# Gate and up maps by Strassen's seven block products, the down map spread between them, its last share and the final norm token-major

## The chip, the cores and the metric

The kernel runs on one core of a Trainium2 chip. The metric is the device time of the whole program in microseconds (us). Three runs of the kernel before took 1119.18, 1119.93 and 1120.37 us, so the median is 1119.93 us.

## What is computed

The reference is one inference step of a two-layer streaming encoder. Every layer is `x = x + mixer(norm(x))`, then `x = x + ffn(norm(x))`; a last norm follows. The part that matters here is the feed-forward map, with `D_MODEL` = 1024 and `D_FF` = 2816:

```
def rmsnorm(x, g):
    xf = x.astype(jnp.float32)
    y = xf * lax.rsqrt(jnp.mean(xf * xf, axis=-1, keepdims=True) + EPS)
    return (y * g.astype(jnp.float32)).astype(x.dtype)

def swiglu(x, w_gate, w_up, w_down):
    return (jax.nn.silu(x @ w_gate) * (x @ w_up)) @ w_down
...
        x = x + y
        x = x + swiglu(rmsnorm(x, norm_ffn[layer]), ffn_gate[layer], ffn_up[layer], ffn_down[layer]).astype(x.dtype)
    return (rmsnorm(x, norm_final), ...
```

The mixer of layer 0 is stick-breaking attention beside a recurrent unit; that of layer 1 subtracts the input from trailing means over 2, 4, 8 and 16 tokens and maps them by groups. 512 prompt tokens and 32 sample tokens go through the same weights, 544 tokens in all. Everything is float32.

## The kernel before

The activations stay on chip, features on partitions: `x` is 128 partitions by 8 feature tiles by 544 tokens. TensorE multiplies in a rounded float32 form, so each float32 factor is split into a rounded part and a rest ("hi" and "lo"), and a product is three passes: hi by hi, hi by lo, lo by hi (`mm3`, L146 to L152, all big maps at line L151). A pass is one matmul for each of two halves of the tokens, 272 columns each (`HALVES`, `HN` = 272).

Weights come in blocks of 128 columns by up to 8 feature tiles (`load_w`, L137 to L144): SP, the sync engine's queue, loads `raw` (512 KB for gate and up), ACT copies it to the rounded `whi` (L141), DVE subtracts for `wlo` (L143). There are three buffers of each.

The feed-forward map (`ffn`, L663) takes the 22 tiles of the hidden width in two blocks of 12 and 10. In a block, each tile gets a gate map and an up map (`ffn_in`, L638; 8 feature tiles x 3 passes x 2 halves = 48 matmuls each). DVE scales the sums with the token norms `rs` (L643, L648), ACT does silu, DVE multiplies (L649), and the result is split into `hh` (ACT, L653) and `hl` (DVE, L654). The down map of the block follows: for each of 8 output tiles the sum over the block's hidden tiles, added to `x` by DVE (`add_x`, L594). In layer 1 the last block runs by two parts of the tokens (`LAST`, 288 and 256 columns), and `after1` (L870 on) works on the final norm tile by tile: squares on ACT (L882), transposes to token-major on TensorE (L903), scaling and output transfers at the end (L906 to L911).

Between the maps, `Norm` (L190) prepares the input of the next one: `split` makes `xh` on ACT and `xl` on DVE (L209), `square` the squares on ACT (L201) and their sum on DVE (L202). `rs` (L228) sums over partitions with one-column matmuls (L224), takes root and reciprocal (L81, L178) and spreads the scales over the partitions with TensorE (L186). In the pooling mixer of layer 1, `pool_out` multiplies with band matrices (L820), DVE adds the result to `x` (L823), and `n3.add(m)` follows; the first gate and up maps of layer 1's feed-forward stand between them.

The order of the work is set by a scheduler on every engine, except on TensorE in attention and in the pooling mixer, where it is the order of the code. POOL builds the band matrices (`band`, L699, and the code behind it, in the stage of attention) and loads the pooling weights `pw` (L734).

## Time and profile before

| | |
|---|---|
| median of three runs | 1119.93 us |
| lowest, highest | 1119.18, 1120.37 us |
| span of the profiled execution | 1118.6 us |
| TensorE (PE) busy | 1098.2 us, 98% |
| VectorE (DVE) busy | 542.5 us, 48% |
| ScalarE (ACT) busy | 400.7 us, 36% |
| GpSimd (POOL) busy | 90.9 us, 8% |
| loaded from memory, stored | 94.88 MB, 4.60 MB |

The profile is of one execution. Its span is what the profiler saw between the first and the last instruction, 1118.6 us; the timed runs are 0.6 to 1.8 us longer, and the profiled execution's own time outside the span is not recorded. PEld is TensorE's loading of the stationary operand, which runs beside the matmuls. "Idle before" is the time in which an engine had nothing to do just before the instructions of a row, with what ended it. A TensorE that is busy all the time need not run at its peak, since matmuls are pipelined: the distance between the starts of two matmuls is the pace, not their duration.

### The profile page before, as it was taken

To read this page: it belongs to the slowest core of one execution; us is meant where nothing else is said; L and a number is where in the kernel's file an instruction comes from. 1 tells how busy PE (TensorE), PEld (TensorE's weight loads), DVE (VectorE), ACT (ScalarE), POOL (GpSimd) and SP (SyncE) were. 2 spreads that over 40 slices of the span, in tenths; PEclk is the share of its full clock that TensorE was granted. 3 is DMA by queue.
4 is the path that set the end of the run, shared out by engine and by line. 5 is a ranking of instruction groups with operands and counts; after the bars stand their busy time and mean duration, and the time that the engine had idled before them with its cause. 6 is when DMAs were issued, how large, how long until landed. Compare 5 with 4: busy or idle time off the path is not lost.

```text
span 1118.6 us, 20133 instructions
## 1 busy us (share of the span) xinstructions
PE 1098.2 (98%) x8591; PEld 1072.5 (96%) x8591; DVE 542.5 (48%) x797; ACT 400.7 (36%) x626; POOL 90.9 (8%) x242
## 2 busy tenths in 40 slices
PE   8989999999999999999999999999999999999997
PEld 7978888899999999999999999999999999999997
DVE  6785667654444342344343455544433224444575
ACT  7555555543322222122232344422222112222454
POOL 5162225400000000000000000000000000000000
PEclk8989999999999999999999999999999999999999
DMA  8412222323232323333322340132222333322364
GB/s 226 130 49 67 68 67 79 97 76 95 76 91 80 91 69 88 95 95 94 93 71 60 94 119 23 43 92 83 88 81 71 88 108 89 94 86 64 108 188 126
DMA packets 183977, 100.78 MB, mean 90 GB/s; under 512 B 4215, under 2 KB 180575, under 8 KB 183888
## 3 DMA queue, kind: packets, MB, share of 16 engines
q1 hardware_dynamic: 182352, 96.88, 29.9%
q0 software_dynamic: 1088, 1.56, 0.5%
q8 instruction: 68, 1.11, 0.4%
q10 hardware_dynamic: 448, 1.05, 0.3%
q14 instruction: 21, 0.17, 0.0%
HBM read 94.88 MB, written 4.60 MB: 89 GB/s over the span
## 4 chain that ended last, share of the span: by engine, by line
PE 89%; DVE 4%; issue 4%; POOL 1%; DMA 1%; ACT 1%; SPq 0%; DVEq 0%; POOLq 0%; ACTq 0%
PE acc L151 82%; DVE sB L390 1%; PE acc L786 1%; DMA raw<-in_hyb_w_in_dram 1%; POOL sA L409 1%; PE z L820 1%; PE sm L820 0%; PE sm L427 0%; DVE sA L391 0%; DVE wlo L143 0%; PE sm L418 0%; DVE tr L339 0%; POOL sB L409 0%; PE sm L903 0%; PE sm L328 0%
## 5 line engine op out<-in xcount | busy, mean ns | idle before, releaser
L141 ACT ACTIVATE whi<-raw 128x1024 fp32r<-128x1024 f32 (+2 forms) x196 | 185.1, 946 | 555.4 <-PE acc L151 537.9
L151 PE MATMUL acc<-xh,whi 128*128 128x272 f32 x1728 | 369.2, 295 | 2.4 <-ACT xh L81 2.4
L151 PE MATMUL acc<-xl,whi 128*128 128x272 f32 x1728 | 363.6, 292 | 0.5 <-DVE xl L209 0.5
L151 PE MATMUL acc<-xh,wlo 128*128 128x272 f32 x1728 | 360.6, 290 | 0.0
L151 PEld LDWEIGHTS acc<-xh,whi 128*128 128x128 f32 x1728 | 273.6, 190 | 9.7 <-issue 5.7
L151 PEld LDWEIGHTS acc<-xl,whi 128*128 128x128 f32 x1728 | 274.1, 191 | 1.0 <-DVE xl L209 0.8
L151 PEld LDWEIGHTS acc<-xh,wlo 128*128 128x128 f32 x1728 | 273.7, 189 | 0.1
L143 DVE TENSOR_TENSOR wlo<-raw,whi 128x1024 fp32r<-128x1024 f32 (+2 forms) x196 | 211.6, 1081 | 91.9 <-ACT whi L141 89.2
L151 PE MATMUL acc<-hh,wlo 128*128 128x272 f32 (+2 forms) x704 | 158.9, 288 | 0.0
L151 PE MATMUL acc<-hl,whi 128*128 128x272 f32 (+2 forms) x704 | 158.8, 288 | 0.0
L151 PE MATMUL acc<-hh,whi 128*128 128x272 f32 (+2 forms) x704 | 158.7, 288 | 0.0
L151 PEld LDWEIGHTS acc<-hl,whi 128*128 128x128 f32 x704 | 115.4, 188 | 0.0
L151 PEld LDWEIGHTS acc<-hh,whi 128*128 128x128 f32 x704 | 115.2, 188 | 0.2 <-issue 0.2
L151 PEld LDWEIGHTS acc<-hh,wlo 128*128 128x128 f32 x704 | 115.2, 188 | 0.1
L648 DVE TENSOR_TENSOR sB<-acc,rs 128x544 f32<-128x544 f32 x44 | 31.9, 725 | 170.3 <-PE acc L151 170.3
L643 DVE TENSOR_TENSOR sA<-acc,rs 128x544 f32<-128x544 f32 x44 | 31.9, 725 | 122.5 <-PE acc L151 118.4
L594 DVE TENSOR_TENSOR x<-x,acc 128x544 f32<-128x544 f32 x32 | 23.1, 721 | 84.1 <-PE acc L151 84.1
L390 DVE TENSOR_TENSOR_SCAN sB<-sB 128x128 f32<-128x128 f32 (+4 forms) x34 | 30.7, 907 | 31.2 <-POOL sB L409 30.8
L653 ACT ACTIVATE hh<-sA 128x544 fp32r<-128x544 f32 x44 | 29.0, 660 | 39.4 <-DVE sA L649 39.4
L775 POOL TENSOR_TENSOR pst<-x,cols 128x120 f32<-128x120 f32 x2 | 1.7, 881 | 444.2 <-DVE x L594 444.2
L654 DVE TENSOR_TENSOR hl<-sA,hh 128x544 fp32r<-128x544 f32 x44 | 31.7, 720 | 5.8 <-ACT hh L653 5.8
L649 DVE TENSOR_TENSOR sA<-sA,sB 128x544 f32<-128x544 f32 x44 | 31.9, 724 | 3.6
(298 smaller groups left out, 901.7 us busy)
## 6 DMA issues: line engine op xcount, KB each, us to landing
raw<-in_ffn_gate_dram SPq DMA_DIRECT2D x44, 512.0 KB, 3.7
raw<-in_ffn_up_dram SPq DMA_DIRECT2D x44, 512.0 KB, 3.8
raw<-in_ffn_down_dram SPq DMA_DIRECT2D x48, 320.0 KB, 3.2
raw<-in_ffn_down_dram SPq DMA_DIRECT2D x32, 384.0 KB, 3.4
raw<-in_hyb_w_in_dram SPq DMA_DIRECT2D x20, 512.0 KB, 3.8
raw<-in_hyb_w_out_dram SPq DMA_DIRECT2D x8, 512.0 KB, 4.1
sA<-in_x_prompt_dram SPq DMA_DIRECT2D x3, 512.0 KB, 4.4
vc<-in_cache_sb_v_dram SPq DMA_DIRECT2D x4, 256.0 KB, 7.1
```

Source lines behind the costliest of these rows:

```text
L141: ac.activation(hi[:, :nk], raw[:, :nk], AF.Copy)
L143: ve.tensor_tensor(lo[:, :nk], raw[:, :nk], hi[:, :nk].bitcast(F32), op=ALU.subtract)
L151: pe.matmul(ps[:, h, : s.stop - s.start], lhsT=a[:, wi, :], rhs=b[:, s], start=first and j == 0, stop=last and j == 2)
L390: ve.tensor_tensor_scan(r, r, r, 1.0, op0=ALU.mult, op1=ALU.min)
L409: gp.affine_select(t[:, N - P :], t[:, N - P :], pattern=[[-1, P]], compare_op=ALU.is_gt, fill=fill, base=0, channel_multiplier=1)
L594: ve.tensor_add(half(x[:, m]), half(x[:, m]), ps[:, :, :HN])
L643: ve.tensor_mul(half(t[0]), ps[:, :, :HN], half(nin.r))
L648: ve.tensor_mul(half(t3), ps[:, :, :HN], half(nin.r))
L649: ve.tensor_mul(t1, t1, t3)
L653: ac.activation(a, t1, AF.Copy)
L654: ve.tensor_tensor(b, t1, a.bitcast(F32), op=ALU.subtract)
L786: pe.matmul(o, lhsT=l[:, c : c + n], rhs=r, start=k % 2 == 0 and j == 0, stop=k % 2 == 1 and j == 2)
```

## The change

The hidden tiles are taken in 11 pairs. For a pair, the weights of gate (and of up, in the same tiles, `u` = 0 and 1) are seen as 2 x 2 blocks: two hidden tiles by two halves of the 8 feature tiles. The activations are 2 x 2 blocks too: two halves of the features by two halves of the tokens. Strassen's scheme makes the four blocks of the result from seven block products instead of eight. The factors are sums of blocks:

- Of the weights: `a11`, `a12`, `a22` are plain blocks; `t1` and `t3` are two blocks added by the transfer itself (a load on SP, then an adding load issued by POOL onto the same tile, L814 and L816 of the new file); `t2` and `t4` are added by DVE (L824). All seven are split into hi and lo (ACT L799, DVE L801).
- Of the activations: class `Forms` makes seven forms for each norm, instead of one split; `put` splits a form into its rounded part (ACT, L288, L291) and its rest (DVE, L289, L292).

A product is 4 feature tiles x 3 passes = 12 matmuls of 272 columns (L905) for gate and for up; a pair has 7 x 12 x 2 = 168. The kernel before had 192. The sums of products are formed in the accumulators, with copies by ACT (L912 to L918) and by DVE from L916 to L936.

The down map no longer waits for a block: after products 3 to 10 of a pair come eight sums (`one`, L961), each over the four hidden tiles finished last, for one output tile and one half of the tokens, added to `x` in 272 columns (L964). The last four hidden tiles of layer 0 follow after the last pair, with the next norm; those of layer 1 are multiplied the other way round (`final`): hidden tiles stationary, weight rows of 512 columns moving, tokens on partitions, on top of `x` transposed into the accumulator. The final norm then is a square with sum over the row, a root, and one scaling.

Weights now live in 17 slots of 128 x 1024, taken and given back by a list that counts products; the adding loads and DVE's sums use slots as well. The order on TensorE is that of the code in all of the feed-forward map: the token norms of layer 0 stand before the fifth product of the first pair (gate and up counted apart), those of layer 1 after the sixth, `t2` by `n2`. The band matrices are built in the second pair, and memory pools are laid out anew.

Two kernels in numbers: 8372 matmuls before, 7762 now.

The core of the diff, in pieces. `after1` and the code of the old final norm are removed and not shown:

```diff
+    class Forms(Norm):
+        names = ("b11", "n1", "n2", "b21", "t3", "t4", "b22")
+        def __init__(self, gcol, t0):
+            super().__init__(gcol)
...
+        def add(self, k):
+            j, g = k % 4, col(self.gcol + k)
+            x0, x1 = x[:, k, :HN], x[:, k, HN:]
+            if k < 4:
+                if j % 2 == 0:
+                    self.d[j], self.d[j + 1] = self.tmp(j // 2)
+                d = self.d[j]
+                self.put("b11", j, x0, g)
+                ve.tensor_tensor(d, x0, x1, op=ALU.subtract)
+                self.put("n1", j, d, g)
+            else:
+                d, g0 = self.d[j], col(self.gcol + j)
+                (t, q), (r, _) = self.tmp(2 + 2 * (j % 3)), self.tmp(3 + 2 * (j % 3))
+                ac.activation(t, x1, AF.Copy, scale=g)
+                ve.scalar_tensor_tensor(q, d, g0, t, op0=ALU.mult, op1=ALU.add)
+                self.put("n2", j, q, -1.0)
+                self.put("b21", j, x0, g)
+                ve.scalar_tensor_tensor(r, x[:, j, HN:], g0, t, op0=ALU.mult, op1=ALU.subtract)
+                self.put("t3", j, r, -1.0)
+                ve.scalar_tensor_tensor(q, x0, g, q, op0=ALU.mult, op1=ALU.subtract)
+                self.put("t4", j, q, -1.0)
+                self.put("b22", j, t)
+            self.square(k)
...
+        def split(self, n, *drop):
+            def go():
+                raw = self.raw[n]
+                hi = slot(f"h{n[0]}", F32R)
+                ac.activation(hi, raw, AF.Copy)
+                lo = slot(f"l{n[0]}", F32R)
+                ve.tensor_tensor(lo, raw, hi.bitcast(F32), op=ALU.subtract)
+                self.w[n] = hi, lo
+                self.free(drop, max(self.at[n], clock.pop(), clock.pop()) + 16)
+            self.steps.append((2, go))
+        def blocks(self, n, *which):
+            def go(t):
+                for b, (f, kh) in enumerate(which):
+                    for u, src in enumerate((ffn_gate, ffn_up)):
+                        w = src[self.l][512 * kh : 512 * (kh + 1), P * f : P * (f + 1)].rearrange("(k p) m -> p k m", p=P)
+                        if b:
+                            gp.dma_start(v(t)[:, u], w, accum_op=ALU.add)
+                        else:
+                            nc.sync.dma_start(v(t)[:, u], w)
+                return len(which)
+            self.load(n, go)
+        def add(self, n, a, b, *drop):
+            def go():
+                t = self.raw[n] = slot(f"r{n[0]}")
+                ve.tensor_add(t, self.raw[a], self.raw[b])
+                self.at[n] = max(self.at[a], self.at[b], clock.pop()) + 8
+                self.free(drop, self.at[n])
+            self.steps.append((1, go))
+        def pair(self, fp):
+            n = lambda s: (s, fp)
+            f0, f1 = 2 * fp, 2 * fp + 1
+            self.blocks(n("t1"), (f1, 0), (f1, 1))
+            self.blocks(n("a11"), (f0, 0))
+            self.split(n("a11"))
+            self.split(n("t1"))
+            self.add(n("t2"), n("t1"), n("a11"), n("t1"), n("a11"))
+            self.rows(fp)
+            self.split(n("t2"))
+            self.blocks(n("t3"), (f1, 0), (f0, 0))
+            self.blocks(n("a12"), (f0, 1))
+            self.split(n("a12"))
+            self.add(n("t4"), n("t2"), n("a12"), n("t2"), n("a12"))
+            self.split(n("t3"), n("t3"))
+            self.blocks(n("a22"), (f1, 1))
+            self.split(n("a22"), n("a22"))
+            self.split(n("t4"), n("t4"))
...
+    ORDER = (("a11", "b11"), ("t1", "n1"), ("t2", "n2"), ("a12", "b21"), ("t3", "t3"), ("a22", "t4"), ("t4", "b22"))
...
+            a, b = ORDER[i]
+            (wh, wl), (bh, bl) = [v(w) for w in sup.need((a, fp))], nin.form(b)
+            X, Y = st["xy", u][:, 0, :HN], st["xy", u][:, 1, :HN]
+            Z = st["z", u][:, :HN] if i else None
+            o = (X, Z, X, Y, X, X, Z)[i]
+            first = i in (0, 1, 3)
+            mms = [m for k in range(4) for m in ((wh[:, u, k], bh[:, k]), (wh[:, u, k], bl[:, k]))]
+            mms += [(wl[:, u, k], bh[:, k]) for k in range(4)]
...
+            for n, (lt, r) in enumerate(mms):
+                pe.matmul(o, lhsT=lt, rhs=r, start=first and n == 0, stop=n == 11, skip_group_check=True)
+            if u:
+                sup.done((a, fp))
+            pa, pb, pc = st["abc", u]
+            s, out = st["s"], st["u" if u else "s"]
+            h0, h1 = slice(0, HN), slice(HN, T)
+            if i == 0:
+                ac.activation(pa, X, AF.Copy)
+            elif i == 2:
+                ac.activation(pb, X, AF.Copy)
+            elif i == 3:
+                ve.tensor_tensor(out[:, 0, h0], Y, pa, op=ALU.add)
+            elif i == 4:
+                ac.activation(pc, X, AF.Copy)
+                ve.scalar_tensor_tensor(out[:, 1, h1], Z, -1.0, pc, op0=ALU.mult, op1=ALU.subtract)
+            elif i == 5 and u == 0:
+                ve.scalar_tensor_tensor(s[:, 1, h0], X, -1.0, nin.r[:, h0], op0=ALU.mult, op1=ALU.mult)
+                ve.tensor_mul(s[:, 1, h1], s[:, 1, h1], nin.r[:, h1])
+                act(s[:, 1], s[:, 1], AF.Silu)
+                ve.tensor_mul(s[:, 1], s[:, 1], nin.r)
+            elif i == 5:
+                ve.scalar_tensor_tensor(out[:, 1, h0], X, -1.0, s[:, 1, h0], op0=ALU.mult, op1=ALU.mult)
+                ve.tensor_mul(out[:, 1, h1], out[:, 1, h1], s[:, 1, h1])
+                hidden(out[:, 1], 1)
+            elif i == 6:
+                ve.tensor_tensor(out[:, 0, h1], Z, pb, op=ALU.add)
+                if u == 0:
+                    ve.tensor_mul(s[:, 0], s[:, 0], nin.r)
+                    act(s[:, 0], s[:, 0], AF.Silu)
+                    ve.tensor_mul(s[:, 0], s[:, 0], nin.r)
+                else:
+                    ve.tensor_mul(out[:, 0], out[:, 0], s[:, 0])
+                    hidden(out[:, 0], 0)
...
+            def one(m, hf, s):
+                c = slice(P * (m % 4), P * (m % 4 + 1))
+                ps = small()[:, :HN]
+                for i, f in enumerate(fs):
+                    (wh, wl), (a, b) = sup.row(f, m // 4), hid[f]
+                    for j, (lt, r) in enumerate(((wh, a), (wh, b), (wl, a))):
+                        pe.matmul(ps, lhsT=lt[:, c], rhs=r[:, s], start=i == 0 and j == 0,
+                                  stop=i == len(fs) - 1 and j == 2)
+                xs = x[:, m, s]
+                ve.tensor_add(xs, xs, ps)
...
+                if hf:
+                    if fp == PAIRS:
+                        after(m)
...
+        for fp in range(PAIRS):
+            if fp or not first:
+                prods, sums = strassen(sup, nin, fp, hid), down(fp)
+                for n, f in enumerate(prods):
+                    if n == 4 and fp < len(mid):
+                        mid[fp]()
+                    f()
+                    if n > 2 and sums:
+                        sums.pop(0)()
+        if last:
+            last()
+        if after:
+            for f in down(PAIRS):
+                f()
+        return hid
...
-        first = [], []
-        fg, fu = ffn_in(1, n3, 0, *first)
+        first = {}
+        prods = strassen(supply, n3, 0, first)
         for m in range(4, KD):
             pool_out(m)
+            if m == 7:
+                give(*ptm, *ptb)
+                supply.fill()
             if m in (4, 6):
                 pool_state(m == 6)
-            for s in (fg[m - 4], fu[m - 4]):
-                s()
...
+            prods.pop(0)()
+        prods.pop(0)()
+        prods.pop(0)()
+        scales(n3)
+        for f in prods:
+            f()
...
+        def begin(t):
+            s, _ = TT[t]
+            n = s.stop - s.start
+            if t in (0, 3):
+                fin[t] = small(), small()
+            else:
+                a = accp()
+                fin[t] = a[:, 0], a[:, 1]
+            for m in range(KD):
+                pe.matmul(fin[t][m // 4][:n, P * (m % 4) : P * (m % 4 + 1)], lhsT=x[:, m, s], rhs=ident, is_transpose=True,
+                          start=m % 4 == 0, stop=False, skip_group_check=True)
+        def add(t, fs, stop):
+            s, _ = TT[t]
+            n = s.stop - s.start
+            for h in range(2):
+                for i, f in enumerate(fs):
+                    (wh, wl), (a, b) = sup.row(f, h), hid[f]
+                    for j, (lt, r) in enumerate(((a, wh), (b, wh), (a, wl))):
+                        pe.matmul(fin[t][h][:n], lhsT=lt[:, s], rhs=r, start=False,
+                                  stop=stop and i == len(fs) - 1 and j == 2, skip_group_check=True)
+        def out(t):
+            s, dst = TT[t]
+            n = s.stop - s.start
+            y = slot("y")
+            q = fss[:n, 3 * t : 3 * t + 3]
+            for h in range(2):
+                ac.activation(y[:n, 512 * h : 512 * (h + 1)], fin[t][h][:n], AF.Square, accum_out=q[:, h : h + 1])
+            ve.tensor_add(q[:, 2:3], q[:, 0:1], q[:, 1:2])
+            act(q[:, 2:3], q[:, 2:3], AF.Sqrt, bias=eps[:n], scale=1.0 / D)
+            ve.reciprocal(q[:, 2:3], q[:, 2:3])
+            for h in range(2):
+                c = slice(512 * h, 512 * (h + 1))
+                ve.scalar_tensor_tensor(y[:n, c], fin[t][h][:n], q[:, 2:3], grow[:n, c], op0=ALU.mult, op1=ALU.mult)
+                (ac if h else nc.sync).dma_start(dst[:, c], y[:n, c])
+            give(y)
...
+        phase("sqrt_and_others")
+        for t in range(3):
+            begin(t)
+            add(t, fs[:-1], False)
+        for t in range(3):
+            add(t, fs[-1:], True)
+            out(t)
+        for t in range(3, 5):
+            begin(t)
+            add(t, fs, True)
+            out(t)
+    with tc.manual_schedule(engines={mybir.EngineType.PE}):
+        final(supply, ffn(supply, n3, first=first))
```

Two places show how instructions move. The first is DVE in the middle of layer 0's feed-forward map. Before, one hidden tile (`wlo` is the rest of a weight block, `sA`, `sB`, `hl` are the hidden tile's):

```order
L143 TENSOR_TENSOR wlo_584_4239<-raw_582_4235,whi_583_4237 128x1024
L654 TENSOR_TENSOR hl_568_4111<-sA_561_4049,hh_567_4110 128x544
L643 TENSOR_TENSOR sA_573_4169<-acc_569_4114,rs_480_3251 128x544
L143 TENSOR_TENSOR wlo_589_4297<-raw_587_4293,whi_588_4295 128x1024
L648 TENSOR_TENSOR sB_578_4227<-acc_574_4172,rs_480_3251 128x544
L649 TENSOR_TENSOR sA_573_4169<-sA_573_4169,sB_578_4227 128x544
```

Now, a part of one pair (`lt1` is the rest of `t1`, `rt1` the tile that the adding load writes, `rt2` the raw sum `t2`, `l3` a rest of the down map's rows, `s` and `u` the pair's gate and up):

```order
L916 TENSOR_TENSOR u_691_4700<-acc_696_4718,a_697_4719 128x272
L964 TENSOR_TENSOR x_128<-x_128,sm_718_4897 128x272
L824 TENSOR_TENSOR rt2_716_4892<-rt1_704_4742,ra11_707_4774 128x1024
L801 TENSOR_TENSOR lt1_715_4890<-rt1_704_4742,ht1_714_4888 128x1024
L919 SCALAR_TENSOR_TENSOR s_690_4699<-z_705_4748,c_695_4704 128x272
L964 TENSOR_TENSOR x_128<-x_128,sm_719_4925 128x272
L922 TENSOR_TENSOR s_690_4699<-s_690_4699,rs_519_3336 128x272
L919 SCALAR_TENSOR_TENSOR u_691_4700<-z_706_4761,c_699_4721 128x272
L964 TENSOR_TENSOR x_128<-x_128,sm_723_4959 128x272
L801 TENSOR_TENSOR l3_721_4953<-r3_717_4894,h3_720_4951 128x1024
```

The adds to `x` and the combining of products now stand in one queue behind `rt2` and `lt1`, which read what the adding load wrote.

The second place is DVE at the end of layer 1's pooling mixer, from its last feature tile to the token norms (the two reciprocals, `rt`). Before (`nacc` is the sum of squares, `xl` the rest of the activations):

```order
L823 SCALAR_TENSOR_TENSOR x_122<-z_951_7642,cols_121,x_122 128x272
L823 SCALAR_TENSOR_TENSOR x_122<-sm_952_7643,cols_121,x_122 128x272
L209 SCALAR_TENSOR_TENSOR xl_954_7653<-x_122,cols_121,xh_953_7652 128x544
L202 TENSOR_TENSOR nacc_894_7272<-nacc_894_7272,nsq_955_7656 128x544
L178 RECIPROCAL rt_958_7703<-rt_958_7703 128x4
```

Now the last 12 of the 25 rows from the last adds to `x` to the last rest of the form `n2` (`t3`, `t4`, `b22` are rests of other forms, `tmp` sums of them; `lt1` and `rt2` belong to the second pair):

```order
L292 SCALAR_TENSOR_TENSOR n2_1128_7991<-tmp_1160_8107,n2_1127_7990 128x272
L313 SCALAR_TENSOR_TENSOR tmp_1147_8052<-x_128,cols_127,tmp_1147_8052 128x272
L292 SCALAR_TENSOR_TENSOR t3_1132_8000<-tmp_1161_8108,t3_1131_7999 128x272
L801 TENSOR_TENSOR lt1_1181_8212<-rt1_1175_8185,ht1_1180_8210 128x1024
L824 TENSOR_TENSOR rt2_1182_8214<-rt1_1175_8185,ra11_1176_8190 128x1024
L308 SCALAR_TENSOR_TENSOR tmp_1168_8158<-tmp_1118_7949,cols_127,tmp_1168_8158 128x272
L311 SCALAR_TENSOR_TENSOR tmp_1169_8159<-x_128,cols_127,tmp_1168_8158 128x272
L289 TENSOR_TENSOR b22_1135_8008<-tmp_1168_8158,b22_1135_8008 128x272
L218 TENSOR_TENSOR nacc_1095_7715<-nacc_1095_7715,nsq_1170_8174 128x544
L313 SCALAR_TENSOR_TENSOR tmp_1160_8107<-x_128,cols_127,tmp_1160_8107 128x272
L292 SCALAR_TENSOR_TENSOR t4_1134_8005<-tmp_1147_8052,t4_1133_8004 128x272
L292 SCALAR_TENSOR_TENSOR n2_1128_7991<-tmp_1168_8158,n2_1127_7990 128x272
```

The second pair's weight work and the rests of `t3` and `t4` now stand ahead of the last `n2`, which the products `t2` by `n2` read.

## Rows read from the trace of the kernel before

**Rows 1.** Page, part 1: span; busy us, share and count of each engine
```profile
span 1118.6 us, 20133 instructions
...
PE 1098.2 (98%) x8591; PEld 1072.5 (96%) x8591; DVE 542.5 (48%) x797; ACT 400.7 (36%) x626; POOL 90.9 (8%) x242
```

**Rows 2.** Page, part 4: chain of waits by line
```profile
PE acc L151 82%; DVE sB L390 1%; PE acc L786 1%; DMA raw<-in_hyb_w_in_dram 1%; POOL sA L409 1%; PE z L820 1%; PE sm L820 0%; PE sm L427 0%; DVE sA L391 0%; DVE wlo L143 0%; PE sm L418 0%; DVE tr L339 0%; POOL sB L409 0%; PE sm L903 0%; PE sm L328 0%
```

**Rows 3.** Chain of waits in order: start us, us, engine, tile, line, count
```profile
279.45 389.67 PE acc L151 x3087
...
712.69 344.33 PE acc L151 x2706
```

**Rows 4.** Windows, mid feed-forward: busy us (count) per engine; PEclk, DMA share, GB/s
```profile
600.00:640.00 40.00, 40.00 (x321) 40.00 (x320) 16.90 (x24) 14.04 (x20) 0.00 (x0) 1.00 0.29 81
```

**Rows 5.** Timeline of PE, two stretches: start us, us, engine line op out<-in
```profile
1059.76 0.29 PE L151 MATMUL acc<-hh,wlo 128*128 128x288 f32 x1
...
1061.62 0.30 PE L151 MATMUL acc<-hl,whi 128*128 128x288 f32 x1
...
1083.76 0.28 PE L151 MATMUL acc<-hh,whi 128*128 128x256 f32 x1
...
1085.89 0.28 PE L151 MATMUL acc<-hh,whi 128*128 128x256 f32 x1
```

**Rows 6.** Lines by form: op out<-in count | busy us, mean ns | idle before
```profile
L143 DVE TENSOR_TENSOR wlo<-raw,whi 128x1024 fp32r<-128x1024 f32 x116 | 141.7, 1224 | 24.3 <-ACT whi L141 21.9
...
L648 DVE TENSOR_TENSOR sB<-acc,rs 128x544 f32<-128x544 f32 x44 | 31.9, 725 | 170.3 <-PE acc L151 170.3
...
L202 DVE TENSOR_TENSOR nacc<-nacc,nsq 128x544 f32<-128x544 f32 x21 | 15.1, 718 | 0.0
...
L823 DVE SCALAR_TENSOR_TENSOR x<-z,cols,x 128x272 f32<-128x272 f32 x8 | 4.0, 497 | 2.1 <-PE z L820 1.9
...
L681 DVE TENSOR_TENSOR x<-x,acc 128x288 f32<-128x288 f32 x8 | 3.6, 445 | 2.0 <-PE acc L151 2.0
...
L734 POOL DMA_DIRECT2D pw<-in_pool_w_dram x4 | 3.0, 761 | 11.5 <-PE z L529 11.5
```

**Rows 7.** DMA issues: out<-in queue op count, KB each, median us to landing
```profile
raw<-in_ffn_gate_dram SPq DMA_DIRECT2D x44, 512.0 KB, 3.7
...
pw<-in_pool_w_dram POOLq DMA_DIRECT2D x4, 256.0 KB, 4.9
...
out_dram<-sA ACTq DMA_DIRECT2D x2, 256.0 KB, 3.2
```

**Rows 8.** Chain of waits, end of layer 1's pooling mixer
```profile
702.14 0.54 PE sm L799 x4
702.68 1.51 PE acc L151 x12
704.19 0.43 PE z L820 x4
...
705.64 4.72 PE acc L151 x36
```

**Rows 9.** Windows, from the pooling mixer into the feed-forward map of layer 1
```profile
688.00:700.00 12.00, 12.00 (x94) 11.05 (x94) 10.21 (x19) 7.08 (x12) 1.04 (x2) 1.00 0.03 8
700.00:712.00 12.00, 11.43 (x93) 10.97 (x92) 6.52 (x13) 4.95 (x10) 1.00 (x2) 1.00 0.03 6
712.00:724.00 12.00, 12.00 (x83) 11.79 (x84) 5.56 (x7) 5.78 (x8) 0.00 (x0) 0.86 0.28 82
```

**Rows 10.** Timeline, token norms of layer 1 (idle before and its releaser in brackets)
```profile
711.76 1.28 ACT L75 ACT_TABLE_LOAD   x1
711.87 0.82 PE L186 MATMUL z<-ident,rt 128*128 128x128 f32 x5 [0.57 <-DVE rt L178]
```

**Rows 11.** Timeline, end of the program
```profile
1110.09 0.28 PE L151 MATMUL acc<-hh,wlo 128*128 128x256 f32 x1
...
1113.51 1.01 ACTq L911 DMA_DIRECT2D out_dram<-sA  x2
```

More of the change, by code (lines that the diff above doesn't have):

```diff
@@ L267 @@
     rsv = half(rs)
-    kcs = [big.tile([P, 512], F32, tag=f"kc{i}", name=nm("kc")) for i in range(2)]
+    kcs = [lp.tile([P, 512], F32, tag=f"kc{i}", name=nm("kc")) for i in range(2)]
     bdr, bdi = [t.rearrange("p (c o) -> p c o", c=4) for t in kcs]
@@ L363 @@
                           cache_k[0, 0, P * t : P * (t + 1)].rearrange("t h d -> t (h d)"))
[L364 removed]
+    vc = [lp.tile([P, 512], F32, tag=f"vc{t}", name=nm("vc")) for t in range(4)]
     for t in range(4):
@@ L632, with fb, slot @@
     v_out()
+    lg.__exit__(None, None, None)
+    lp2 = ctx.enter_context(tc.tile_pool(name="lp2", bufs=1, side="left", reuse_waits="tile"))
+    def fb(i, n):
+        return lp2.tile([P, 2176 if i == 12 else 1088], F32, tag=f"fb{i}", name=nm(n))
+    spare, held = [(0, i) for i in range(6)], {}
+    clock = [0]
+    def slot(n, dt=F32):
+        spare.sort()
+        when, i = spare.pop(0)
+        t = (sl if i < 6 else sl2).tile([P, 1024], dt, tag=f"w{i}", name=nm(n))
+        held[id(t)] = t, i
+        clock.append(when)
+        return t
@@ L777 @@
     a2 = n2.acc
-    ptm = [scr(("sA", "sA", "sA", "sB", "sB")[t]) for t in range(5)]
+    ptm = [slot("ptm") for t in range(5)]
+    supply = Supply(1)
+    supply.fill()
     def pool_in(pi, t, i):
```

411 lines of the change are left out of this document (227 added, 184 removed).

## The prediction, made before the changed kernel ran

> **What bounds the kernel now.** I read the page's first part, then the chain of waits, then windows of the feed-forward stretches, then the two places where the order of work changes. TensorE is busy 1098.2 of 1118.6 us, and VectorE 542.5 [rows 1]. A high busy share alone can be a stalled pipeline, so the chain matters more: 82% of it is one line, L151, the big maps [rows 2], and it runs through both feed-forward maps in two unbroken pieces [rows 3]. In the window from 600 to 640 us TensorE is never idle at the full granted clock (2.4 GHz), while VectorE is busy 16.90 of 40 us and the DMA engines 0.29 [rows 4]. There the time is a number of matmuls times a pace: 389.67 / 3087 = 0.126 us in layer 0, 344.33 / 2706 = 0.127 us in layer 1 [rows 3]. I take 0.127. What is removed there is worth its full time, as long as VectorE and the transfers keep up.
>
> **The saving.** 192 gate and up matmuls a pair become 168, so 24 x 11 pairs x 2 layers = 528 fewer, all of 272 columns: 528 x 0.127 = **-67.1 us**. Weight loads fall by as many, since there is one for each matmul before and after (x8591 of both in [rows 1]), so the pace should not change.
>
> **The last share of layer 1.** Its matmuls had 288 and 256 columns. 15 starts of the one kind lie 1.86 us apart, 0.133 each; 19 of the other 2.13 us, 0.118 [rows 5]. That is 0.00046 us a column, so 512 columns are estimated at 0.118 + 256 x 0.00046 = 0.236. Before: 576 x 0.127 + 240 x (0.133 + 0.118) = 133.4 us for the whole down map. Now 18 hidden tiles the old way, 864 x 0.127 = 109.7, and 5 token tiles x 2 halves x 4 hidden tiles x 3 passes = 120 x 0.236 = 28.3: 138.0, so +4.6. The 40 transposes stay 40. The way out is 1118.6 - 1110.4 = 8.2 us after the last product [rows 11]; the new one (two squares, root, reciprocal, two scalings of 512 columns, a 256 KB store of 3.2 us [rows 7]) should be about a microsecond shorter. Together **+3.5** (0 to 6).
>
> **Steady pairs, cover by VectorE.** A pair is 168 products and 96 down matmuls, 264 x 0.127 = 33.5 us of TensorE. VectorE gets, at row prices [rows 6]: 9 rests of 128x1024 (seven, and two of down rows) and 2 sums at 1.22, 8 adds to x and 10 combinations of 272 columns at 0.45 (the 288-column row), 6 operations of 544 at 0.725: 13.5 + 8.0 + 4.4 = 25.9 us, 77% of the pair. It fits, but no longer loosely. The adds to x release the two accumulators that the down sums alternate between, so a VectorE that waits more than some 3 us stops TensorE.
>
> What can make it wait is the adding load, an operation that the trace does not have. The loop is: the rest of `t4` is made and frees a slot; SP loads the plain blocks of the next `t1` into it; POOL adds the others; then `rt2` and `lt1` may run; and between these and the next rest of `t4` VectorE has 10 operations of 1024, 6 of 544 and 11 of 272 columns, 12.2 + 4.4 + 5.0 = 21.6 us. So base load plus adding load may take 33.5 - 21.6 = **11.9 us** before the loop, not TensorE, sets the pair. The base is 3.7 us (512 KB from SP, here two of 256 KB) [rows 7]. For the adding loads the lower bound is the same 3.7, the nearest row of POOL's own queue is `pw`: 256 KB, 0.76 us of POOL each to issue [rows 6] and 4.9 us to land [rows 7]. Upper bound: the two after one another, 9.8. So 7.4, 8.6 or 13.5 us; I take two that overlap, 0.8 + 4.9, hence 9.4 with the base, inside the loop by 2.5 us. Transfers grow too: seven block loads of 0.5 MB and about 1 MB of down rows a pair, 4.5 MB in 33.5 us, 134 GB/s beside the 81 of [rows 4], and each adding load also reads its target; latencies may stretch. I put **+2.5** on twenty pairs.
>
> The trace has 4.9 us for a 256 KB load that POOL issues [rows 7]. The Trainium skill, "DMA: Bandwidth & Descriptors" (section "Anatomy of one DMA"), gives such transfers a fit of 2.0 us plus the bytes over 436 thousand a microsecond, 2.6 us here as an estimate, well under the row; by it base and adding load would be some 7 us and the loop loose; the steady term would be 0 and the sum 1083.8. The row decides. Against the change speaks the same page's "Rules for kernel authors": an accumulating DMA reads its destination and writes it later, and only GpSimd can issue it; no run yet shows what that costs.
>
> **First pair of layer 0: +6** (2 to 12). Before, the token norms lay between products that were ready. Now they stand at a fixed place; their chain costs TensorE what it does at layer 1, 0.57 us for the reciprocal [rows 10] and as much for the sums; a table load of 1.28 us [rows 10] delays ACT's copy of `t2`; the first `t3` waits for an adding load that stands in POOL's queue with the band matrices; and the forms are new VectorE work just there. About 1.4 + 0.8 + 2 + 1.3, rounded up for a clock that may drop.
>
> **End of layer 0: +1.5** (0 to 4). An output tile of the last share is now 24 matmuls, 3.0 us, instead of 60. VectorE has two adds, a rest of 0.79, the squares' sum 0.72 and in the later tiles a `pwl` of 0.7 for each, 3.1 us. It ends a little late.
>
> **From the pooling mixer into layer 1: +20** (8 to 27). This is the expensive place. In the kernel before VectorE is already busy 10.21 of 12 us there [rows 9], and TensorE loses little, 0.57 us, and 0.14 of the next 12 us to the clock [rows 9, 10]. Now VectorE's queue holds, from the sum `rt4` to the last rest of `n2`, 36 operations: 7 of 1024 columns at 1.22, 3 sums of squares at 0.72, and 26 of 272 at 0.50 (the L823 row) [rows 6]: 8.6 + 2.2 + 13.0 = 23.7 us. TensorE has in the same stretch a state transpose of 0.54, a product 1.51, `pool_out` 705.64 - 704.19 = 1.45, and another product 1.51 [rows 8]: 5.0 us. It must then wait for `n2`, 18.7 us if VectorE starts no earlier; I take 16.5, since some rows can run ahead, 1.4 for the norms, and 2.1 for the clock: after a pause of half a microsecond it was granted 0.86 over 12 us [rows 9], and this pause is far longer. The adding load for the second pair ends in 9.4 us after the last `pool_out`, earlier than VectorE reaches its rest, so it does not decide here.
>
> **Sum.** -67.1 + 3.5 + 2.5 + 6 + 1.5 + 20 = -33.6. From the profiled 1118.6 us: 1085.0. The median of the runs lies 1.3 us above the span: **1086 us**.
>
> **Rivals.**
> 1. Everything beside the two norms hides: the forms are made early because VectorE has gaps before the mixer ends, and the steady term is 0. For it: 48% busy overall [rows 1]. Against: 10.21 of 12 just there [rows 9]. Then -67.1 + 3.5 + 3 + 7 = -53.6: **1066**.
> 2. The loop is a little too long in the steady pairs: base and adding load 12.5 to 13.3 us, excess 0.6 to 1.4 x 20 pairs = 12 to 28 us on top of the forecast less its 2.5: **1096 to 1112**. For it: the upper bound of 13.5; against: two loads in different halves of a slot need not queue.
> 3. Slower than before: the same loop, longer. It breaks even at an excess of (33.6 + 2.5) / 20 = 1.8 us, at 13.7 us for base plus adding load. At 15.5 us the pair is 3.6 us too long, 72 - 36 = +36: **1156**. For it: an operation without any row, on a queue whose only larger loads take 4.9 us, with targets that must be read too. Against: nothing in the rows is above 13.5.
> 4. The change does not do what it says: the pace per matmul rises because each weight is loaded for one product of 272 columns and the accumulators alternate more often. Against: one weight load for each matmul already. The feed-forward maps keep some 5700 matmuls; at 0.133 us they cost 34 us more, and nothing is gained: **1120**.
>
> **How the numbers follow.** The forecast 0.45 (1074 to 1096), rival 1 0.22, rival 2 0.17, rival 3 0.12, rival 4 0.04. No change means within 0.2%, 2.2 us, about what a measurement of this kernel can tell. Faster is the first three, 0.84; rival 4 straddles and gives 0.03 to the same; slower 0.13. The range goes from 1064, under rival 1, to 1118, over rival 2: it leaves out rival 3 and little else.
>
> **What would show it.** In the profile after: PE around 0.127 us a matmul and idle under 1 us in 40 in the steady pairs, with VectorE near 77%; a gap of some 16 us on TensorE ended by a rest of `n2` on VectorE after layer 1's last `pool_out`; adding loads of about 5 to 6 us. Wrong: gaps of some microseconds in every pair, ended by adds to x, with VectorE itself waiting for a DMA into `rt1` (rivals 2 and 3); or no gap at the mixer's end (rival 1); or a pace above 0.13 without gaps (rival 4).

## The result, and the profile after

The changed kernel took 1206.5 us (median of four runs), 1.078 times the kernel before (95% interval 1.076 to 1.080). The forecast was 1086 us, with a range up to 1118: it was wrong in sign. Rival 3, the loop through the adding loads, comes nearest, with 1156, but not by its sum: it needed 15.5 us for the two loads in the loop, and they took 10.2 (below).

The page after: span and busy time, the granted clock and the DMA share in 40 slices, the queue of POOL's transfers (packets, MB, share of 16 engines' span), and the chain of waits by engine and by line. It answers to [rows 1] and [rows 2]. Below it are the clock and the chain by engine of the kernel before.

```profile
span 1206.0 us, 19831 instructions
PE 1084.3 (90%) x7971; PEld 1036.7 (86%) x7971; DVE 762.9 (63%) x1214; ACT 496.2 (41%) x825; POOL 209.8 (17%) x331
...
PEclk8989999998898999999989899689888999899999
DMA  8322233308464655566644421254645556466422
...
q0 software_dynamic: 47696, 25.16, 16.2%
...
PE 51%; DMA 20%; DVE 14%; issue 7%; ACT 5%; POOL 1%; SPq 1%; DVEq 0%; POOLq 0%; ACTq 0%
PE acc L905 18%; PE sm L961 14%; PE acc L167 9%; DMA rt<-in_ffn_up_dram 9%; DMA ra<-in_ffn_up_dram 7%; DMA r<-in_ffn_down_dram 3%; PE z L905 3%; DVE la L801 2%; DVE lt L801 2%; PE acc L1222 1%; DVE rt L824 1%; ACT ha L799 1%; DVE sB L473 1%; PE acc L1112 1%; DVE l L801 1%
```

```profile
PEclk8989999999999999999999999999999999999999
...
PE 89%; DVE 4%; issue 4%; POOL 1%; DMA 1%; ACT 1%; SPq 0%; DVEq 0%; POOLq 0%; ACTq 0%
```

TensorE fell from 98% to 90% busy [rows 1], and its clock, full in the kernel before through both feed-forward maps but for one stretch [rows 9], now drops again and again from the tenth slice on. In the chain, TensorE's share is 51% (89% before) and transfers hold 20%, among them `rt`, the tiles of the adding loads. The windows show the same by stage: nine pairs of layer 0, the end of the pooling mixer, and ten pairs of layer 1 (us, busy time and count by engine; then clock, DMA share, GB/s).

```profile
317.00:656.00 339.00, 309.77 (x2328) 305.31 (x2329) 213.27 (x318) 120.04 (x170) 46.64 (x36) 0.95 0.56 125
751.00:777.00 26.00, 12.83 (x56) 11.36 (x54) 20.79 (x37) 14.60 (x28) 2.65 (x2) 0.63 0.41 96
785.00:1151.00 366.00, 332.48 (x2490) 327.89 (x2488) 227.72 (x338) 129.99 (x184) 49.85 (x39) 0.94 0.55 123
```

In these pairs TensorE is idle 29 + 34 = 63 us, and the clock takes 0.05 x 339 + 0.06 x 366 = 39 us more. Before, both were zero in such a window [rows 4]. VectorE, at 63% (213.27 / 339), is not full. What ended TensorE's waits (total us, times, longest), the two largest entries of each window, layer 0 first:

```profile
PE acc L905 <- ACT c L918: 8.5, 3, 3.5
PE sm L961 <- ACT hh L942: 8.5, 4, 2.9
...
PE sm L961 <- ACT hh L942: 13.5, 5, 3.2
PE acc L905 <- DVE u L916: 7.8, 3, 5.2
```

With the rests `hl`, 29 of the 63 us end with a hidden tile; most of the others end with a copy or a combination of products (`c`, `u`).

A pair should take 33.5 us. I read it off the starts of VectorE's first combination of each pair (L916): from the fourth to the eleventh pair of layer 0 it is 655.5 - 391.7 = 263.8 us, 37.7 a pair on average. The pairs alternate: 36.5, 42.3, 33.1, 40.9, 33.1, 41.9 and 36.0 us. The chain of waits through the long pair of 42.3 us (start us, us, what) shows two adding loads one after the other:

```profile
431.12 0.45 DVE x L964
...
432.40 5.82 DMA rt<-in_ffn_up_dram
...
439.27 0.39 ACT c L918
439.70 2.57 PE acc L905 x12
...
449.40 5.50 DMA rt<-in_ffn_up_dram
...
460.88 0.82 PE sm L961 x2
```

The first (`t1`) lands at 438.2. ScalarE's copy of it stands ahead of the copy `c`, and the product that waits for `c` starts at 439.7. The second (`t3`) lands at 454.9; its copy and one more on ScalarE stand ahead of the hidden tile's steps, and TensorE waits for that tile (`hh`, `hl`) until 460.9. TensorE at these two places:

```profile
439.70 1.66 PE L905 MATMUL acc<-t,ha 128*128 128x272 f32 x8 [2.61 <-ACT c L918]
...
459.80 0.39 PE L961 MATMUL sm<-hh,h 128*128 128x272 f32 x1 [2.87 <-ACT hh L942]
```

Windows just behind each wait show what the clock then takes: the granted clock is 0.59 and 0.50, with TensorE busy all the time.

```profile
439.70:443.50 3.80, 3.80 (x19) 3.80 (x20) 2.72 (x6) 0.23 (x1) 0.00 (x0) 0.59 0.73 214
...
461.00:464.20 3.20, 3.20 (x14) 3.20 (x15) 1.31 (x2) 0.00 (x0) 0.00 (x0) 0.50 0.27 77
```

The timeline of VectorE and SP around the first load (idle before, and what ended it, in brackets):

```profile
426.72 1.22 DVE L801 TENSOR_TENSOR lt<-rt,ht 128x1024 fp32r<-128x1024 f32 x1
...
428.00 0.37 SPq L816 DMA_DIRECT2D rt<-in_ffn_gate_dram  x1
...
438.31 1.23 DVE L824 TENSOR_TENSOR rt<-rt,ra 128x1024 f32<-128x1024 f32 x1 [6.76 <-DMA rt<-in_ffn_up_dram]
...
444.90 1.23 DVE L801 TENSOR_TENSOR l<-r,h 128x1024 fp32r<-128x1024 f32 x1 [2.48 <-ACT h L799]
...
460.74 1.22 DVE L801 TENSOR_TENSOR lt<-rt,ht 128x1024 fp32r<-128x1024 f32 x1
```

At 426.7 VectorE makes the rest of `t4`, which frees a slot; at 428.0 SP loads the plain blocks; at 438.3, after 6.76 us of idling, VectorE may add `rt2`; at 460.7 comes the next rest of `t4`. This is the loop of the forecast, in this turn 34.0 us long: 10.3 us of loads and 23.7 us in VectorE's queue, where the forecast had 21.6 us of work and no waits (2.48 us for a copy at 444.9 is one). In each of the seven turns between 390.6 and 648.3 SP's load follows the rest of `t4` within 0.1 us. But the turns take 36.2, 34.0, 39.8, 34.2, 38.7, 35.3 and 39.7 us: one of 34.0 alone would cost half a microsecond. In the next one, of 39.8 us, the second adding load stands in the loop as well. It lands at 494.2, VectorE then makes the rest of `t3`, and the rest of `t4` comes behind it:

```profile
495.69 1.23 DVE L801 TENSOR_TENSOR lt<-rt,ht 128x1024 fp32r<-128x1024 f32 x1 [1.95 <-ACT ht L799]
...
500.52 1.23 DVE L801 TENSOR_TENSOR lt<-rt,ht 128x1024 fp32r<-128x1024 f32 x1
...
501.82 0.37 SPq L816 DMA_DIRECT2D rt<-in_ffn_gate_dram  x1
```

From the landing of `t1` at 472.1 to the end of that rest it is 29.7 us.

### The profile page after: what moved, and what is told of

Same layout as the page of the kernel before. It is cut to its first block, busy times and chain, and to the rows that moved or that the text cites. A ratio compares the mean times of both kernels' runs of the same rounds, so it can differ in the third digit from the quotient of the medians.

```text
span 1206.0 us, 19831 instructions
## 1 busy us (share of the span) xinstructions
PE 1084.3 (90%) x7971; PEld 1036.7 (86%) x7971; DVE 762.9 (63%) x1214; ACT 496.2 (41%) x825; POOL 209.8 (17%) x331
## 3 DMA queue, kind: packets, MB, share of 16 engines
q0 software_dynamic: 47696, 25.16, 16.2%
HBM read 124.76 MB, written 4.60 MB: 107 GB/s over the span
## 4 chain that ended last, share of the span: by engine, by line
PE 51%; DMA 20%; DVE 14%; issue 7%; ACT 5%; POOL 1%; SPq 1%; DVEq 0%; POOLq 0%; ACTq 0%
PE acc L905 18%; PE sm L961 14%; PE acc L167 9%; DMA rt<-in_ffn_up_dram 9%; DMA ra<-in_ffn_up_dram 7%; DMA r<-in_ffn_down_dram 3%; PE z L905 3%; DVE la L801 2%; DVE lt L801 2%; PE acc L1222 1%; DVE rt L824 1%; ACT ha L799 1%; DVE sB L473 1%; PE acc L1112 1%; DVE l L801 1%
## 5 line engine op out<-in xcount | busy, mean ns | idle before, releaser
L961 PE MATMUL sm<-hh,h 128*128 128x272 f32 x640 | 192.0, 300 | 39.4 <-ACT hh L942 30.5
L961 PE MATMUL sm<-hl,h 128*128 128x272 f32 x640 | 191.3, 299 | 8.2 <-DVE hl L943 8.2
L961 PE MATMUL sm<-hh,l 128*128 128x272 f32 x640 | 189.1, 295 | 1.3 <-DVE l L801 1.3
L814 POOL DMA_DIRECT2D rt<-in_ffn_gate_dram x44 | 56.7, 1289 | 651.0 <-PE z L905 210.6
L799 ACT ACTIVATE ht<-rt 128x1024 fp32r<-128x1024 f32 x88 | 91.3, 1053 | 183.5 <-DMA rt<-in_ffn_up_dram 176.2
L961 PEld LDWEIGHTS sm<-hh,h 128*128 128x128 f32 x640 | 125.7, 196 | 44.8 <-ACT hh L942 33.1
L801 DVE TENSOR_TENSOR lt<-rt,ht 128x1024 fp32r<-128x1024 f32 x88 | 108.6, 1234 | 43.4 <-ACT ht L799 40.9
L961 PEld LDWEIGHTS sm<-hl,h 128*128 128x128 f32 x640 | 126.1, 197 | 10.9 <-DVE hl L943 10.9
L961 PEld LDWEIGHTS sm<-hh,l 128*128 128x128 f32 x640 | 126.1, 197 | 1.5 <-DVE l L801 1.5
L964 DVE TENSOR_TENSOR x<-x,sm 128x272 f32<-128x272 f32 x176 | 75.7, 431 | 68.7 <-PE sm L961 68.5
L905 PE MATMUL acc<-b,ha 128*128 128x272 f32 x704 | 107.4, 296 | 9.6 <-DVE u L926 9.2
L905 PEld LDWEIGHTS acc<-b,ha 128*128 128x128 f32 x704 | 97.1, 195 | 10.8 <-DVE u L926 9.9
L801 DVE TENSOR_TENSOR la<-ra,ha 128x1024 fp32r<-128x1024 f32 x66 | 80.5, 1222 | 28.8 <-ACT ha L799 23.2
L801 DVE TENSOR_TENSOR l<-r,h 128x1024 fp32r<-128x1024 f32 x44 | 53.9, 1224 | 68.4 <-ACT h L799 65.1
L799 ACT ACTIVATE ha<-ra 128x1024 fp32r<-128x1024 f32 x66 | 69.7, 1058 | 63.5 <-DMA ra<-in_ffn_up_dram 53.7
L824 DVE TENSOR_TENSOR rt<-rt,ra 128x1024 f32<-128x1024 f32 x44 | 54.2, 1232 | 65.1 <-DMA rt<-in_ffn_up_dram 48.2
L799 ACT ACTIVATE h<-r 128x1024 fp32r<-128x1024 f32 x44 | 46.6, 1059 | 111.8 <-DMA r<-in_ffn_down_dram 107.0
L167 PE MATMUL acc<-xh,whi 128*128 128x272 f32 x320 | 75.7, 318 | 2.3 <-ACT xh L97 2.3
L814 POOL DMA_DIRECT2D rt<-in_ffn_up_dram x44 | 74.6, 1695 | 14.2 <-DMA rt<-in_ffn_up_dram 13.1
L905 PE MATMUL acc<-n,ht 128*128 128x272 f32 x352 | 63.2, 329 | 10.9 <-ACT n L291 6.6
L167 PE MATMUL acc<-xl,whi 128*128 128x272 f32 x320 | 68.4, 295 | 0.5 <-DVE xl L227 0.5
L167 PE MATMUL acc<-xh,wlo 128*128 128x272 f32 x320 | 67.9, 294 | 0.0
```

Of the source, the lines that this page charges most:

```text
L167: pe.matmul(ps[:, h, : s.stop - s.start], lhsT=a[:, wi, :], rhs=b[:, s], start=first and j == 0, stop=last and j == 2)
L799: ac.activation(hi, raw, AF.Copy)
L801: ve.tensor_tensor(lo, raw, hi.bitcast(F32), op=ALU.subtract)
L814: gp.dma_start(v(t)[:, u], w, accum_op=ALU.add)
L824: ve.tensor_add(t, self.raw[a], self.raw[b])
L905: pe.matmul(o, lhsT=lt, rhs=r, start=first and n == 0, stop=n == 11, skip_group_check=True)
```

## The experiments

Four groups ran on one chip each: late_sums to slots18, gate to ve_sums_gate, second_plain and ve_sums_gate_rs, and the last two. The chip of the changed kernel's first runs is not on record. The kernel before is the same everywhere within 0.2%; the changed one is not, as the last group shows, so where a few us matter I compare within a group or say that the chips differ. "Pair" is the mean from the fourth to the eleventh pair of layer 0.

| kernel | median us | ratio to before | pair us |
|---|---|---|---|
| changed | 1206.5 | 1.078 (1.076 to 1.080) | 37.7 |
| late_sums | 1216.6 | 1.089 (1.083 to 1.095) | 38.9 |
| no_add | 1153.9 | 1.029 (1.026 to 1.031) | 35.4 |
| late_no_add | 1124.1 | 1.004 (1.003 to 1.006) | 34.1 |
| slots18 | 1209.0 | 1.080 (1.077 to 1.083) | 37.6 |
| gate | 1214.1 | 1.086 (1.083 to 1.089) | 38.5 |
| ve_sums | 1114.7 | 0.996 (0.995 to 0.998) | 33.1 |
| pool_sums | 1125.0 | 1.005 (1.004 to 1.007) | 33.7 |
| ve_sums_gate | 1107.7 | 0.990 (0.987 to 0.993) | 33.1 |
| second_plain | 1162.7 | 1.038 (1.036 to 1.039) | 35.6 |
| ve_sums_gate_rs | 1112.8 | 0.994 (0.993 to 0.995) | 33.1 |
| after_again | 1216.9 | 1.086 (1.085 to 1.088) | 38.7 |
| gate_again | 1211.6 | 1.082 (1.080 to 1.083) | 38.2 |

**late_sums**

```diff
-                    if n > 2 and sums:
+                    if n > 5 and sums:
```

> The eight sums of the down map start after the seventh product of a pair (gate and up counted apart) instead of the fourth; nothing else changes. Two theories. A, two causes: in every odd pair the first sum reads hidden tiles that VectorE and ScalarE finish only some 8 us after the last product of the pair before, since rests of weight blocks stand between; in the changed kernel TensorE waits about 40 us in all for hh and hl (21 in layer 0, 19 in layer 1), and each wait is followed by a stretch at half clock, about half of the 53 us that the clock cost in both feed-forward maps. A expects these waits to vanish: 1206 - 40 - 25 = about 1140. B, one cause: the loop through the adding load and VectorE's queue is longer than a pair, and the waits for hh are only the place where the lag shows. B expects the waits to move to other products and the time to stay above 1185.

No gain: 1216.6. The waits for `hh` fell from 31 to 4 us, but waits for the copy `b` on ScalarE took their place (46.5 us), and from the fifth pair on all are now about 38 us long. The chain at one of them:

```profile
563.50 1.02 PE z L905 x8
564.53 3.06 DMA rt<-in_ffn_gate_dram
568.16 0.89 POOL rt L814
569.04 5.53 DMA rt<-in_ffn_up_dram
574.65 1.07 ACT ht L799
575.75 1.24 DVE lt L801
577.00 1.06 ACT ht L799
...
578.40 3.09 PE acc L905 x12
```

A product frees a slot, the plain load of `t3` takes it, the adding load follows, then ScalarE's and VectorE's split; ScalarE's queue holds the copy of the product behind that split, and TensorE starts its next product at 578.4, 14 us after it freed the slot. So theory A falls as it stood: taking the wait for the hidden tile away gains nothing while a longer one stands behind it.

**no_add** and **late_no_add**

```diff
...
-                        if b:
-                            gp.dma_start(v(t)[:, u], w, accum_op=ALU.add)
-                        else:
+                        if not b:
...
```

> The adding loads of t1 and t3 are left out (these two factors are then one block instead of a sum of two, so the result differs); the plain loads and all else stay. A expects the waits that follow a late rt2 to go (c, u, s and x on TensorE's list, some 43 us in both layers) with their share of the clock, 20 to 25: about 1140, with the waits for hh and hl still there. B expects nearly the whole excess over the forecast to go: 1100 or less. If the adding loads don't matter, above 1190.

> Both edits: the down map's sums three products later, and no adding loads (t1 and t3 are one block each, so the result differs). A expects both groups of waits to go, 1206 - 83 - 50 = about 1075, and mean clock near 1 in the pairs. B expects the same time as without the adding loads alone, within 10 us.

1153.9 and 1124.1. (In both, and in second_plain, the two factors are not the full sums, so these kernels only time the parts.) Without the adding loads the late sums are worth 30 us, with them nothing. Neither theory had this: the longer wait hides the shorter. The 1075 of theory A was not reached; the pairs of late_no_add are 1 us over TensorE's own time, and what is left stands mainly at the stage borders (below).

**slots18** (one more slot; room for it from the third copy of a pair, now in the first one's buffer, and from smaller tiles elsewhere)

```diff
...
-    spare += [(0, i) for i in range(6, 17)]
+    spare += [(0, i) for i in range(6, 18)]
...
```

> One more slot for weight blocks, 18 instead of 17 (room is made by giving the third copy of a pair the first one's buffer, and by three small tiles). The adding loads stay. If the loop is closed by slots coming free late (the plain load of t1 waits for the rest of t4), A and B both expect earlier loads and less waiting for rt2: 1160 to 1185. If the list hands out the new slot elsewhere, or the loop closes in another way, 1200 to 1210.

1209.0: one slot more does not open the ring. That fits its last case; whether the new slot went elsewhere or another wait closed the ring is open.

**second_plain**

```diff
-                            gp.dma_start(v(t)[:, u], w, accum_op=ALU.add)
+                            gp.dma_start(v(t)[:, u], w)
```

> GpSimd's loads of t1 and t3 write over the tile instead of adding to it (t1 and t3 are then their second block alone, so the result differs); when they run, what they wait for and how much they move from memory is unchanged. If the adding itself, with its reading of the target, is what is slow, the landing falls from 4.6 and 5.6 us toward the 3.0 and 3.5 us of SP's loads and the time falls to about 1160 to 1180. If the cost is that a second load stands behind the first in the loop, whatever it does, the time stays at 1200 to 1215.

1162.7, as the first case expected: the adding itself costs. The second load in line costs less: with it left out altogether (no_add, on another chip) the kernel takes 1153.9. The changed kernel's block loads (KB each, us to landing) and POOL's issue of the second (count | busy us, mean ns | idle before):

```profile
rt<-in_ffn_gate_dram SPq DMA_DIRECT2D x44, 256.0 KB, 3.0
rt<-in_ffn_up_dram SPq DMA_DIRECT2D x44, 256.0 KB, 3.5
rt<-in_ffn_gate_dram POOLq DMA_DIRECT2D x44, 256.0 KB, 4.6
rt<-in_ffn_up_dram POOLq DMA_DIRECT2D x44, 256.0 KB, 5.6
```

```profile
L814 POOL DMA_DIRECT2D rt<-in_ffn_up_dram x44 | 74.6, 1695 | 14.2 <-DMA rt<-in_ffn_up_dram 13.1 <-issue 1.0
```

The same in second_plain, with its POOL queue:

```profile
q0 software_dynamic: 8272, 25.16, 7.5%
...
rt<-in_ffn_gate_dram POOLq DMA_DIRECT2D x44, 256.0 KB, 3.6
rt<-in_ffn_up_dram POOLq DMA_DIRECT2D x44, 256.0 KB, 3.6
```

```profile
L814 POOL DMA_DIRECT2D rt<-in_ffn_up_dram x44 | 33.0, 750 | 21.6 <-DMA rt<-in_ffn_up_dram 16.4 <-issue 3.5 <-DVE u L919 0.6
```

The same bytes (25.16 MB in this queue) went in 8272 packets instead of 47696 and took 7.5% of the DMA engines' time instead of 16.2%; POOL needed 0.75 us instead of 1.70 for the second issue, and the second landing came after 3.6 instead of 5.6 us. Two adding steps that land up to 2 us sooner in 22 pairs are some 88 us of landing; 44 to 54 us of the time went, by which run of the changed kernel it is set against (1206.5 or 1216.9). The plain loads beside them gained too: SP's loads of `ra` landed after 3.1 and 3.8 us instead of 3.8 and 4.3. How the 44 to 54 us divide between the adding loads' own landing, their issue and these neighbours was not separated.

**ve_sums** and **pool_sums**: no adding loads, but the full result. The blocks are loaded once each, and the down sums come late as in late_sums. In pool_sums the sums `t1` and `t3` have `eng=gp`.

```diff
...
-            self.blocks(n("t1"), (f1, 0), (f1, 1))
+            self.blocks(n("a21"), (f1, 0))
+            self.blocks(n("a22"), (f1, 1))
...
+            self.add(n("t1"), n("a21"), n("a22"), eng=ve)
...
+            self.add(n("t3"), n("a21"), n("a11"), n("a21"), n("a11"), eng=ve)
...
-                    if n > 2 and sums:
+                    if n > 5 and sums:
```

> No adding loads: the blocks a11, a12, a21 and a22 are each loaded once by SP, t1 and t3 are sums made by VectorE like t2 and t4 (4 sums of 128x1024 a pair instead of 2), and the down map's sums start three products later, as in late_sums. The result is complete. The loop theory (adding loads of 10 us, twice a pair, in a chain with both queues) expects about the time without adding loads, 1124, plus little, since a pair has some 5 us of VectorE free: 1120 to 1135. If VectorE's own load is the limit, 2 x 1.22 us x 22 pairs come on top: about 1175.

> As ve_sums, but the sums t1 and t3 are made by GpSimd. Its 128x128 sums took 0.46 us in the kernel before; eight times that is 3.7 us as an estimate, 7.4 us a pair on an engine with nothing else to do. The chain of base load and sum is then 3.7 + 3.7 instead of 10.2 us, VectorE has no more work than in the changed kernel. Loop theory: 1115 to 1130. If sums on GpSimd slow VectorE or take over 6 us each, above 1150.

ve_sums, 1114.7, is 0.4% faster than the kernel before (ratio 0.995 to 0.998), and its pairs take 33.1 us, the time of their 264 matmuls. Its window from 400 to 640 us:

```profile
400.00:640.00 240.00, 233.98 (x1850) 233.02 (x1849) 181.78 (x263) 97.75 (x137) 2.90 (x4) 0.99 0.34 100
```

TensorE is idle 6 us, VectorE busy 76%, the clock 0.99, and memory traffic is down to 100 GB/s. VectorE's own load, with 54 us more work than in the changed kernel by the forecast's prices, is not the limit. Compared with late_sums (1216.6) two things changed at once: the sums moved to an engine, and fewer blocks are loaded (124.76 MB read from memory in late_sums, 90.16 in ve_sums). Their shares were not separated. pool_sums is 10 us slower; a sum on GpSimd takes 2.44 us, under the estimate:

```profile
L824 POOL TENSOR_TENSOR rt<-ra,ra 128x1024 f32<-128x1024 f32 x44 | 107.5, 2442 | 643.2 <-DMA ra<-in_ffn_up_dram 297.1 <-PE sm L962 79.3 <-DVE rt L824 60.4
```

**ve_sums_gate**, **gate**, and the changed kernel and gate again on one chip: at the end of layer 1's pooling mixer the weight work is ordered behind the last `n2`: VectorE's sums and rests behind its rest, ScalarE's copies behind its rounded part.

```diff
...
+    def behind(i, e):
+        if gates:
+            tc.add_manual_dep(i.ins, gates[e].name, nosync, reason="gate")
...
-                ve.tensor_add(t, self.raw[a], self.raw[b])
+                behind(ve.tensor_add(t, self.raw[a], self.raw[b]), 1)
...
```

> ve_sums with the weight work of the pooling mixer's end behind the last n2, as in gate. Expected 4 to 12 us under ve_sums if the order there costs what the forecast said; the same time if it is only waited for later.

> Changed kernel, but at the end of layer 1's pooling mixer the weight work (rt4, lt3, lt4, la22, la11, lt1, rt2: 7 operations of 128x1024 on VectorE, and ScalarE's copies) is put behind the last rest of n2. If VectorE's queue of 23.7 us is what TensorE waits for there, 8.6 us of it now stand behind: the products t2 by n2 start earlier, with less half clock, 4 to 12 us less in all (about 1198). If the same work is only waited for later (t3, a22, t4), within 2 us of the changed kernel.

> The changed kernel itself, beside gate on one chip. The gate kernel took 1214 us on a chip on which the changed kernel had not run; in its layer 0, where each engine's instructions are the same as in the changed kernel, it was already 10 us longer. If pairs that are bound by the adding loads differ from chip to chip, this run is again within 1200 to 1216, and what counts is the difference to gate_again.

> The gate kernel on the same chip as after_again. If the order at the end of the pooling mixer costs what ve_sums_gate suggests (7 us under ve_sums), 4 to 12 us under after_again. If the later adding load of the second pair takes it back, no difference or slower.

ve_sums_gate: 1107.7, 7 us under ve_sums on the same chip. gate alone came out at 1214.1 and looked like a loss; beside the changed kernel on one chip it is 5.3 us faster (1211.6 against 1216.9). The stage from the mixer's first product to the spread norms shrank from 63.0 to 56.7 us there. The changed kernel itself took 1206.5 in its first runs and 1216.9 in these. In ve_sums_gate layer 1 no longer waits at all in its steady pairs (window 800 to 1040):

```profile
800.00:1040.00 240.00, 240.00 (x1914) 239.82 (x1914) 189.25 (x268) 100.42 (x141) 0.55 (x1) 1.00 0.33 95
```

**ve_sums_gate_rs** (ve_sums_gate with the token norms of both layers later; the piece for layer 0)

```diff
...
-                    if n == 4 and fp < len(mid):
+                    if n == 8 and fp < len(mid):
...
```

> ve_sums_gate with the token norms of both layers later in TensorE's fixed order (after the eighth product of the first pair instead of after the fourth and sixth; the scales are first read at the eleventh). In ve_sums_gate TensorE waits 3.4 and 4.0 us for their reciprocals. If VectorE is then only late by its queue, 5 to 10 us less: 1098 to 1103. If the wait moves on to the products behind, no change from 1108.

1112.8, on another chip than ve_sums_gate (1107.7): no gain shown. The fastest version is ve_sums_gate, 1.0% under the kernel before.

## Why the prediction was wrong, point by point

- **The pace and the saving held.** 264 matmuls in 33.1 us are 0.125 each (0.127 was taken), as soon as nothing else holds the pair. The -67.1 us were there, but ve_sums_gate kept only 11.6 of them (1119.3 to 1107.7 on its chip): with its pairs at 33.1 us, the rest goes outside the steady pairs.
- **The step that failed** is the one on steady pairs: "So base load plus adding load may take 33.5 - 21.6 = **11.9 us** before the loop, not TensorE, sets the pair", and the +2.5 drawn from it. The loads took 10.2 us (428.0 to 438.2), near the 9.4 expected and under the bound, and still the pairs of both layers lost some 100 us (63 idle, 39 by the clock): about every second pair takes 40 us or more, most of the others 33 to 37. The runs show what the bound left out. It summed VectorE's operations as if none waited (23.7 us in one turn of the loop, 29.7 in the next, instead of 21.6). It followed one adding load through VectorE, while a pair has two, and both also hold ScalarE's queue, where the copies and the hidden tile stand behind them (the chain above; late_sums). And it left out that in every second pair the first down sums need the hidden tiles of the pair just ended, which are ready 10 to 13 us after its last product, while the first sum comes after 6 us of new products (30 us in late_no_add against no_add).
- **The price of the adding load** was bounded by plain loads. It landed in 4.6 and 5.6 us, inside the bounds taken from [rows 7]; but as plain loads the same two take 3.6 each, and a kernel with plain ones is 44 us or more faster (second_plain). The fit of the Trainium skill, "DMA: Bandwidth & Descriptors" (section "Anatomy of one DMA"), 2.6 us for 256 KB by my estimate, is under both measurements.
- **The clock** had 2.1 us in the forecast, at one place. Waits in the long pairs, most of 2 to 3 us and the longest 5.2, with a granted clock of 0.5 to 0.6 for some us behind them, brought the granted clock to 0.95 and 0.94 over the pairs, 39 us.
- **The pooling mixer's end** was right in size: +20 forecast. From the first pooled product (714.1) to the spread norms (777.6) it takes 63.5 us, where the kernel before took 669.1 to 712.7 [rows 3], 43.6: +19.9. TensorE waits there for the form `n2`, and the granted clock is 0.63 in the window 751 to 777:

```profile
768.08 0.59 PE L905 MATMUL acc<-n,ht 128*128 128x272 f32 x1 [5.63 <-ACT n L291]
```

  In its parts it was off, so that the agreement is partly luck: in that window TensorE idles 13.2 us, where 17.9 were forecast, and the clock, forecast at 2.1, takes more. And the forecast said that the second pair's adding load "does not decide here". It does stand in the chain:

```profile
757.47 5.59 DMA rt<-in_ffn_up_dram
...
763.17 1.06 ACT ht L799
...
764.26 1.23 DVE lt L801
...
769.20 0.36 DVE n L292
```

  The weight work behind that load stands ahead of the last forms in VectorE's queue. But the load is not the main part: without adding loads (no_add) the same stage takes 61.8 us. The gate runs, in which the weight work comes after `n2`, took 5 to 7 us out of it.
- **First pair and end of layer 0** were too small. From the first product to the second pair's first combination 50 us went by (267.3 to 317.3), where 270 matmuls need 34: +16 against +6; the longest wait there, 6.4 us, is for a combination of products on VectorE (L926). From the last pair's first combination to the mixer 58.6 us (655.5 to 714.1), where 336 need 42.7: +16 against +1.5, with two waits of 3.8 and 4.7 us for `hh`, the hidden tile again. What orders VectorE's work there was not tested by a run.
- **The last share** was right as far as the ledger can tell: the way out takes 1206.0 - 1199.4 = 6.6 us, 1.6 less than before [rows 11], the 512-column matmuls start 0.23 us apart (0.236 was taken), and with some 3 for it the ledger gives -67 + 3 + 16 + 16 + 20 + 100 = +88, measured +87. It is a remainder of rounded terms, so it does not measure the 3.

## What to carry to other kernels

When matmuls are taken away from a kernel that is bound by TensorE, the rest of a round becomes a ring of loads, splits and queues, and it must be summed as a ring: every wait inside it, every transfer that stands in it twice, and the results that the next round needs early. An engine at 63% busy can hold up TensorE when the next operation in its queue waits for a load; the same engine at 76%, without such loads, did not. Where a sum of weight blocks can be had from a transfer or from an engine that is 63% busy, the engine was the better place here (1114.7 against 1216.6 us, both with late sums; the engine's version also reads each block only once).
